# Scores of a gated recurrence by matmuls of 32 array columns, in place of 128, 64 and 32

## The chip, the cores and the metric

One core of a Trainium2 chip runs one kernel. The metric is device time in microseconds (us) of one execution. TensorE (PE) multiplies and loads its weights (PEld), VectorE (DVE), ScalarE (ACT) and GpSimd (POOL) do the rest, SyncE (SP) issues most of the DMAs.

## What is computed

The reference is an encoder trunk of two layers on 1024 tokens of width 1024, in float32. Both layers hold a bidirectional gated linear recurrence in chunks (`bidirectional_gated_scan`): four heads of 128 keys and 256 values in layer 0, twelve heads of 128 and 128 in layer 1. Cut to what matters here:

```python
b = jnp.cumsum(log_g, axis=2)                      # within a chunk
s = einsum('bnthk,bnshk->bnhts', q * exp(b - ref), k * exp(ref - b))
s = where(tril, s, 0.0)                            # scores within a chunk
o = einsum(s, v) + einsum(q * exp(b), state)       # per direction
```

The forward result and the flipped backward one are added, less the diagonal that both hold. The change touches `s` alone.

## The kernel before

**Staging.** The input projection runs in blocks of 128 channels and 512 tokens (`project`, L217 to L220; three matmuls per 128 rows of the contraction, on values split in two exact parts). The mixers come one after another: four pairs of attention heads (to about 517 us), four `GlaHead`s (to about 950 us), twelve `HgrnHead`s (from about 1010 us). While a head's core runs, `merge` lays projection blocks and output products beside it by fixed windows. That list is the order of priority; the tile framework orders each engine's instructions by it ahead of time, and lets an instruction that its plan finds ready pass one that it finds not ready. On the chip every engine's program is fixed.

**The core of a head** (`ScanHead.core`) does, for direction d (1 backward, 0 forward) and half hf of the tokens, in the order (1,1), (1,0), (0,0), (0,1): `prep` (gate products on ACT, DVE and POOL), `keys` (transposes at L760, state products at L769), `scores`, and for d = 0 then `output` (L820 to L824). So `scores` is called 4 times in each of 16 heads, 64 times.

**`scores`** makes, for 4 tiles of 128 tokens, X[s, t] of 128 by 128, in one PSUM bank of tag "s" (two buffers). Within 32 tokens the operands `ki`, `qi` serve; between the two 32-token pieces of a half tile `k1`, `q1` (scaled by products of gates, against overflow); between the two 64-token halves of a tile `k2`, `q2`. L794 multiplies each whole tile: 4 matmuls of 128 weight columns by 128 moving columns. L796 writes over the block between the halves (4 of 64 by 64), L801 over the blocks between the pieces (8 of 32 by 32, alternately at two of the four places of 32 array columns that lie 64 apart). Then one instruction moves the bank to `S`: for d = 1 a copy on ACT (L804), for d = 0 a masked copy on DVE (L806). All operands are float32, for which the program on PE holds two weight loads and two matmuls for each matmul of the source: the 256 of L794 stand as 512 in the trace. `S` is read by L820.

Of the kernel before, what the change touches and what calls it, by code (L numbers as in the profile page):

```python
# [55 lines left out]
def merge(*streams):  # L56
    """Units of several streams side by side; a stream (units, start, end) is spread over that part of the whole."""
    todo = []
    for units, a, b in streams:
        todo += [(a + (b - a) * (i + 0.5) / len(units), n, u) for n, (i, u) in enumerate(enumerate(units))]  # L60
    return [u for _, _, u in sorted(todo, key=lambda t: t[0])]


def emit(units):
    """Runs the units; the weights of each block load while the block before it is in use."""
    blocks, first = [], {}
    for i, u in enumerate(units):
        b = getattr(u, "block", None)
        if b and b not in blocks:
            blocks.append(b)  # L70
            first[b] = i
    for i, u in enumerate(units):
        b = getattr(u, "block", None)
        if b:
            for nb in blocks[blocks.index(b):][:2]:
                if nb is b or not any(getattr(v, "fence", False) for v in units[i:first[nb]]):
                    nb.load()
        u()


class Block:
    """Columns f0..f0+n of a projection; evac(ps, half) takes each half of the tokens out of PSUM."""
# [17 lines left out]
class Phase:  # L100
    """A pool that holds one phase's tiles."""
# [14 lines left out]
class Trunk:  # L116
# [15 lines left out]
    def set_mode(self):  # L132
        """Loads the table set that has both exp and ln."""
        self.guard = self.nc.scalar.preload_act_table_set("natural_log_exp_and_others").ins

    def act(self, *args, **kw):
        """An exp or ln; it keeps clear of the sigmoid batches."""
        with self.tc.issue_after(self.guard):
            self.last = self.nc.scalar.activation(*args, **kw).ins  # L139

    def sigmoids(self, fns, after):
        """A batch of sigmoids behind the last exp and behind `after`, then back to exp and ln."""
        prev = [i for i in (self.last, after) if i is not None]
        with self.tc.high_priority(offset=3000):
            for f in fns:
                with ExitStack() as st:
                    for p in prev:
                        st.enter_context(self.tc.issue_after(p))
                    prev = [f().ins]
            with self.tc.issue_after(prev[0]):  # L150
                self.set_mode()
# [4 lines left out]
    def load_w(self, w, f0, n):  # L156
        """Columns f0..f0+n of w [D, F] as two exact parts, a list of [P, n] for each k tile."""
# [27 lines left out]
    def load_wout(self, w, f0, nb, c0, nc_):  # L185
        """Rows f0..f0+128 nb, columns c0..c0+nc_ of w as two exact parts [P, nb, nc_]; nb nc_ = 1024."""
        h = self.wp.tile([P, nb, nc_], F32R, tag="woH", name="woH", bufs=1)
        lo = self.wp.tile([P, nb, nc_], F32R, tag="woL", name="woL", bufs=1)
        for g in range(2):
            raw = self.wp.tile([P, HALF], F32, tag="wraw", name="wraw", bufs=2)  # L190
            if nb == 2:
                src, hs, ls = w[f0 + g * P:f0 + (g + 1) * P, c0:c0 + nc_], h[:, g, :], lo[:, g, :]
            else:
                gs = slice(g * HALF, (g + 1) * HALF)
                src, hs, ls = w[f0:f0 + P, gs], h[:, 0, gs], lo[:, 0, gs]
            self.nc.sync.dma_start(raw, src)
            with self.tc.high_priority(offset=3000):
                self.nc.scalar.copy(hs, raw)  # L198
                self.nc.vector.tensor_tensor(ls, raw, hs.bitcast(F32), op=ALU.subtract)  # L199
        return h, lo  # L200

    def project(self, w, hf, m):
        """Channel-major projection of one half of the tokens: PSUM [m, 512]."""
# [19 lines left out]
    def out_units(self, w, ys, f0, hf, held):  # L223
        """z += y @ w[f0:...] for 4 token tiles; ys = [(yH, yL)] blocks of 128 features [P, 512 tokens]."""
# [29 lines left out]
    def final_units(self, w, f0, ys, norm, banks, reload):  # L254
        """The last product of the layer for one half of the tokens: z and y @ w meet in PSUM, for norm(i, halves).

        Returns a function of the half: the units that take z there for the first two tiles, and the others.
        """
# [46 lines left out]
    def transpose_x(self, i):  # L305
        """Token tile i of x, in z [P, D] -> columns of x^T, in two exact parts."""
# [12 lines left out]
    def after_x(self, fn):  # L319
        """A unit whose work on ACT and DVE stays behind the transposed input."""  # L320
        def run():
            with self.tc.issue_after(self.lastact), self.tc.issue_after(self.lastdve):
                fn()
        return run

    def ln_params(self, pool, tags, gain, bias):
        """Gain and bias of a layer norm on all partitions, in halves."""
# [8 lines left out]
    def layer_norm(self, pool, i, params, direct=False, src=None):  # L336
        """LayerNorm of token tile i into z; z, or the halves `src`, hold (alpha x + y) / alpha."""
# [27 lines left out]
class Item:  # L365
    """One unit of the mixers: the first `ne` of its projection blocks come early, the others late."""
# [10 lines left out]
    def units(self, ns, evac=None):  # L377
        """Units of the blocks ns whose values are not parked."""
# [13 lines left out]
    def spill(self, pool, tag, bufs, which):  # L392
        """Units for the (block, half) pairs of `which` ahead of this item's phase; the values wait in DRAM."""
# [37 lines left out]
class AttnPair(Item):  # L431
    """Two heads of the dilated attention.

    Tokens are taken as t = 4 j + r. A tile of queries has one residue r and one half h of the j; it meets
    A: the four residues of its own half, B: its own residue in the other half,
    C: the 16 nearest j of the other half in every residue (its own one masked, as B has it).
    """
# [12 lines left out]
    @staticmethod  # L450
    def edge(g):
        """The 16 positions of half g next to the other half."""
        return slice(112, 128) if g == 0 else slice(0, 16)
# [63 lines left out]
    def core(self):  # L517
# [4 lines left out]
        def strip(j):  # L522
            """Bias of every block, each run of keys reversed."""
# [119 lines left out]
class ScanHead(Item):  # L643
    """Bidirectional gated linear recurrence of one head: channel-major operands, token-major values."""
# [9 lines left out]
    def raw(self, dst, tag, bufs, scale=1.0):  # L654
        """Evacuation as it is, but for a factor."""
# [10 lines left out]
    def ev_v(self, vb):  # L666
        """Evacuation of values."""
# [8 lines left out]
    def tok_v(self, vt, hf, vb):  # L676
        """Values [128 channels, 512 tokens] -> token-major."""
# [8 lines left out]
    def prep(self, d, hf):  # L686
        """Gate products of 512 tokens for direction d (0 forward, 1 backward)."""
# [65 lines left out]
    def keys(self, d, hf):  # L753
        """State increments and states of 4 token tiles."""
# [29 lines left out]
    def scores(self, d, hf):  # L784
        """S^T[s, t] within 4 token tiles, built from three levels of blocks."""
# [5 lines left out]
        X = T.ps.tile([P, 4, P], F32, tag="s", name="s", bufs=2)  # L791
        for t in range(4):
            ts = slice(t * P, (t + 1) * P)
            mm(X[:, t, :], r["ki"][:, ts], r["qi"][:, ts], start=True, stop=True)  # L794
        for t in range(4):
            mm(X[64 * first:64 * first + 64, t, 64 * last:64 * last + 64],  # L796
               r["k2"][:, t].rearrange("p a c -> p (a c)"), r["q2"][:, t].rearrange("p a c -> p (a c)"),
               start=True, stop=True)
        for n in range(8):
            s0, t0 = 64 * (n % 2) + 32 * ev, 64 * (n % 2) + 32 * od  # L800
            mm(X[s0:s0 + 32, n // 2, t0:t0 + 32], r["k1"][:, n, :], r["q1"][:, n, :], start=True, stop=True)  # L801
        dst = self.S[:, hf * 4:hf * 4 + 4, :]
        if d == 1:
            nc.scalar.copy(dst, X)  # L804
        else:
            nc.vector.copy_predicated(out=dst, mask=T.mask.unsqueeze(1).broadcast_to([P, 4, P]), data=X)  # L806

    def output(self, hf):
        """o^T of 4 token tiles, normalised and gated, in two exact parts."""
# [84 lines left out]
class GlaHead(ScanHead):  # L894
# [20 lines left out]
    def ev_lr(self, ps, hf):  # L915
        """The low-rank gate inputs of every head, as stacked exact parts."""
# [8 lines left out]
    def gates(self):  # L925
        """Up-projection of the gates, as stacked exact parts."""
# [26 lines left out]
    def activate(self, d):  # L953
        """SiLU of the output gates."""
# [35 lines left out]
class HgrnHead(ScanHead):  # L990
# [25 lines left out]
    def out_half(self, hf):  # L1016
        """The output product of two heads, beside the second one."""
        return super().out_half(hf) if self.mate else []
# [11 lines left out]
    def activate(self, d):  # L1030
        """Sigmoids and SiLUs of what direction d needs; the output gate's may come apart."""
# [28 lines left out]
def trunk_kernel(tc, x, w_in_ab, gla_gate_up, gla_gate_bias, gla_norm, w_out_ab, w_in_c, hgrn_lower_bounds,  # L1060
                 hgrn_norm, w_out_c, rel_bias, ln_gain, ln_bias, onehot, ident, mask, out):
    nc = tc.nc
    with ExitStack() as ctx:
# [59 lines left out]
        def bias_line(q):  # L1123
            """Bias and log multiplicity of 512 of the distances."""
# [51 lines left out]
        def step(items, i, after=None, spill=()):  # L1176
            """Item i's core; beside it its late projections, the next item's early ones, the last item's product.

            After the last item come its own product, `after` for the token tiles of each finished half and `spill`.
            """  # L1180
# [66 lines left out]
def shape_constants():  # L1247
    """Tables that depend on the shapes alone."""
# [32 lines left out]
```

## Time and profile before

| | us |
|---|---|
| median of 3 runs (2070.28, 2071.64, 2073.94) | 2071.64 |
| span of the profiled execution | 2070.0 |
| PE busy in it | 2026.0 (98%) |
| DVE busy | 1304.6 (63%) |
| ACT busy | 1012.3 (49%) |
| POOL busy | 308.4 (15%) |

The profiled span is 1.6 us below the median and 0.3 us below the lowest run. "Busy" joins all instructions of an engine; matmuls overlap in the pipeline, so that a duration of 275 ns says little of the pace. The pace is read from starts: how long a run of n equal matmuls takes, less the last one's own duration, over n - 1.

### The profile page before, as it was taken

What the parts mean: (1) busy time and instruction counts of PE and PEld (TensorE: products, weight loads), DVE (VectorE), ACT (ScalarE), POOL (GpSimd) and SP (SyncE); (2) the same over time, 40 slices, a digit from 0 to 9 for tenths busy, and PEclk for the clock granted to TensorE, in tenths of its full rate; (3) what the DMA queues carried; (4) which work ended last, traced back from release to release, by engine and by line L of the source; (5) the groups of instructions that cost most, each with busy time, mean ns of one, the idle gap of its engine ahead of it and who ended that gap; (6) DMA issues with size and microseconds to landing.
All of it is one profiled execution on the core that took longest, in us unless ns stands there. A gap on an engine that the chain in (4) does not pass through costs nothing.

```text
span 2070.0 us, 29623 instructions
## 1 busy us (share of the span) xinstructions
PE 2026.0 (98%) x11103; PEld 1590.7 (77%) x11103; DVE 1304.6 (63%) x2727; ACT 1012.3 (49%) x1844; POOL 308.4 (15%) x838
## 2 busy tenths in 40 slices
PE   8999999999999999998999999999999999999998
PEld 6777676777787878876788788878878887887885
DVE  4677778776676565567675745555664464656467
ACT  4555555543544344344555444435444553544463
POOL 0100000100111011012222111111211111211124
PEclk9999999999999999999999999999999999999999
DMA  5311111211211112111311111111111111111112
GB/s 141 78 35 44 30 40 26 48 52 52 69 36 42 52 32 71 42 51 41 118 37 41 52 46 36 37 57 32 42 61 32 41 36 56 32 42 52 36 52 82
DMA packets 141258, 103.47 MB, mean 50 GB/s; under 512 B 14517, under 2 KB 122933, under 8 KB 141115
## 3 DMA queue, kind: packets, MB, share of 16 engines
q1 hardware_dynamic: 129355, 89.44, 14.7%
q0 software_dynamic: 3968, 9.77, 2.0%
q10 hardware_dynamic: 7792, 2.37, 0.5%
q8 instruction: 87, 1.43, 0.3%
q14 instruction: 56, 0.46, 0.1%
HBM read 93.71 MB, written 7.85 MB: 49 GB/s over the span
## 4 chain that ended last, share of the span: by engine, by line
PE 63%; DVE 4%; ACT 3%; issue 2%; POOL 1%; DMA 0%; DVEq 0%; ACTq 0%; POOLq 0%
PE pj L218 13%; PE pj L219 13%; PE pj L220 13%; PE kv L769 3%; PE s L794 2%; PE po L240 2%; PE po L241 2%; PE po L242 2%; PE s L796 2%; PE o L820 2%; PE o L822 1%; PE o L824 1%; PE tr L760 1%; PE s L801 1%; PE tr L683 1%
## 5 line engine op out<-in xcount | busy, mean ns | idle before, releaser
L218 PE MATMUL pj<-xH,wH 128*128 128x512 f32 x1600 | 649.1, 406 | 3.7 <-ACT vt L490 1.1
L219 PE MATMUL pj<-xL,wH 128*128 128x512 f32 x1600 | 642.9, 402 | 0.0
L220 PE MATMUL pj<-xH,wL 128*128 128x512 f32 x1600 | 640.9, 401 | 0.0
L218 PEld LDWEIGHTS pj<-xH,wH 128*128 128x128 f32 x1600 | 300.9, 188 | 73.8 <-ACT vt L490 2.8
L220 PEld LDWEIGHTS pj<-xH,wL 128*128 128x128 f32 x1600 | 300.9, 188 | 67.0 <-issue 2.4
L219 PEld LDWEIGHTS pj<-xL,wH 128*128 128x128 f32 x1600 | 301.1, 188 | 63.5 <-issue 1.7
L181 DVE TENSOR_TENSOR wL<-wraw,wH 128x512 fp32r<-128x512 f32 x210 | 146.6, 698 | 201.5 <-ACT wH L180 174.4
L180 ACT CAST wH<-wraw 128x512 fp32r<-128x512 f32 x210 | 129.9, 619 | 225.6 <-PE pj L219 191.7
L714 POOL TENSOR_TENSOR eT<-gE 128x16 f32<-128x16 f32 x64 | 36.2, 566 | 1106.6 <-ACT gE L139 1106.6
L245 DVE TENSOR_TENSOR z<-z,po 128x512 f32<-128x512 f32 x200 | 135.9, 683 | 79.9 <-PE po L242 77.8
L240 PE MATMUL po<-woH,yH 128*128 128x512 f32 x336 | 135.9, 409 | 0.9 <-ACT yH L618 0.4
L241 PE MATMUL po<-woL,yH 128*128 128x512 f32 x336 | 133.8, 398 | 1.4 <-DVE woL L199 1.4
L242 PE MATMUL po<-woH,yL 128*128 128x512 f32 x336 | 131.3, 393 | 0.0
L198 ACT CAST woH<-wraw 128x512 fp32r<-128x512 f32 x80 | 47.5, 617 | 94.1 <-PE po L242 43.8
L830 ACT ACTIVATE tmp<-o 128x512 f32<-128x512 f32 x40 | 23.9, 597 | 129.4 <-PE o L822 71.7
L661 ACT ACTIVATE F<-pj 128x512 f32<-128x512 f32 x62 | 36.8, 593 | 94.9 <-PE pj L220 94.9
L769 PE MATMUL kv<-v,k3T 128*128 128x128 f32 (+1 forms) x448 | 79.0, 311 | 1.1 <-ACT k3T L763 0.7
L240 PEld LDWEIGHTS po<-woH,yH 128*128 128x128 f32 x336 | 62.4, 188 | 22.9 <-ACT woH L198 5.3
L694 DVE TENSOR_TENSOR_SCAN g<-restart,g 128x512 f32<-128x512 uint8 x64 | 78.0, 1219 | 1.8 <-ACT g L139 1.2
L241 PEld LDWEIGHTS po<-woL,yH 128*128 128x128 f32 x336 | 63.2, 188 | 16.0 <-DVE woL L199 5.3
L242 PEld LDWEIGHTS po<-woH,yL 128*128 128x128 f32 x336 | 63.2, 188 | 14.0 <-DVE yL L849 1.1
L769 PEld LDWEIGHTS kv<-v,k3T 128*128 128x128 f32 x448 | 61.4, 190 | 16.0 <-ACT k3T L763 7.7
(226 smaller groups left out, 3581.0 us busy)
## 6 DMA issues: line engine op xcount, KB each, us to landing
wraw<-in_w_in_c_dram SPq DMA_DIRECT2D x130, 256.0 KB
wraw<-in_w_in_ab_dram SPq DMA_DIRECT2D x80, 256.0 KB
wraw<-in_w_out_c_dram SPq DMA_DIRECT2D x44, 256.0 KB
wraw<-in_w_out_ab_dram SPq DMA_DIRECT2D x40, 256.0 KB
strip<-line POOLq DMA_DIRECT2D x8, 448.0 KB, 5.3
park<-sp SPq DMA_DIRECT2D x13, 256.0 KB
out_dram<-z SPq DMA_DIRECT2D x6, 512.0 KB
z<-in_x_dram SPq DMA_DIRECT2D x4, 512.0 KB
```

The lines of the kernel that those rows point to most:

```text
L180: self.nc.scalar.copy(h, raw)
L181: self.nc.vector.tensor_tensor(lo, raw, h.bitcast(F32), op=ALU.subtract)
L198: self.nc.scalar.copy(hs, raw)
L218: mm(ps[:m], wH, xH[:, k, :], start=(k == 0), stop=False)
L219: mm(ps[:m], wH, xL[:, k, :], start=False, stop=False)
L220: self.lastmm = mm(ps[:m], wL, xH[:, k, :], start=False, stop=(k == last)).ins
L240: mm(ps, yH[:, ts], h, start=(b == 0), stop=False)
L241: mm(ps, yH[:, ts], lo, start=False, stop=False)
L242: mm(ps, yL[:, ts], h, start=False, stop=(b == nb - 1))
L245: self.nc.vector.tensor_tensor(zs, zs, ps, op=ALU.add)
L694: nc.vector.tensor_tensor_scan(run, T.restart, run, 0.0, op0=M, op1=ALU.add)
L769: nc.tensor.matmul(kv[:, j, :], k3T[:, t, :], self.v[:, hf * 4 + t, :], start=True, stop=True)
```

## The change

`scores` makes the same S from matmuls of 32 weight columns only, 32 of the source for each call instead of 16 (64 weight loads and 64 matmuls on PE instead of 32 and 32). For each tile `far` makes the block between the halves in two strips of 32 by 64, `near` the two blocks between pieces (32 by 32 each), `own` the four blocks on the diagonal, where the strip of the second piece (in the direction's order) takes 64 columns and that of the first 32. No block is written twice. The order in a tile goes round the four places of 32 array columns. The blocks that the mask or the other direction replaces are no longer made. The move to `S` is cut in two, 64 partitions each: one instruction of 4 by 128 columns and one of 4 by 64. Elsewhere only docstrings are gone.

```diff
     def scores(self, d, hf):
...
         X = T.ps.tile([P, 4, P], F32, tag="s", name="s", bufs=2)
+        def block(t, s0, t0, n, k, q):
+            mm(X[s0:s0 + 32, t, t0:t0 + n], k, q, start=True, stop=True)
+        def far(t, i):
+            k2, q2 = (r[x][:, t].rearrange("p a c -> p (a c)") for x in ("k2", "q2"))
+            block(t, 64 * first + 32 * i, 64 * last, 64, k2[:, 32 * i:32 * i + 32], q2)
+        def near(t, i):
+            n = 2 * t + i
+            block(t, 64 * i + 32 * ev, 64 * i + 32 * od, 32, r["k1"][:, n, :], r["q1"][:, n, :])
+        def own(t, i, e):
+            s0 = 64 * i + 32 * e
+            t0, n = (s0, 32) if e == ev else (64 * i, 64)
+            block(t, s0, t0, n, r["ki"][:, t * P + s0:t * P + s0 + 32], r["qi"][:, t * P + t0:t * P + t0 + n])
         for t in range(4):
-            ts = slice(t * P, (t + 1) * P)
-            mm(X[:, t, :], r["ki"][:, ts], r["qi"][:, ts], start=True, stop=True)
-        for t in range(4):
-            mm(X[64 * first:64 * first + 64, t, 64 * last:64 * last + 64],
-               r["k2"][:, t].rearrange("p a c -> p (a c)"), r["q2"][:, t].rearrange("p a c -> p (a c)"),
-               start=True, stop=True)
-        for n in range(8):
-            s0, t0 = 64 * (n % 2) + 32 * ev, 64 * (n % 2) + 32 * od
-            mm(X[s0:s0 + 32, n // 2, t0:t0 + 32], r["k1"][:, n, :], r["q1"][:, n, :], start=True, stop=True)
+            far(t, ev), far(t, od), own(t, last, ev), own(t, last, od)
+            near(t, first), own(t, first, od), near(t, last), own(t, first, ev)
         dst = self.S[:, hf * 4:hf * 4 + 4, :]
-        if d == 1:
-            nc.scalar.copy(dst, X)
-        else:
-            nc.vector.copy_predicated(out=dst, mask=T.mask.unsqueeze(1).broadcast_to([P, 4, P]), data=X)
+        for i in range(2):
+            ss = slice(64 * i, 64 * i + 64)
+            cs = slice(0, P) if i == first else slice(64 * last, 64 * last + 64)
+            if d == 1:
+                nc.scalar.copy(dst[ss, :, cs], X[ss, :, cs])
+            else:
+                mask = T.mask[ss, cs].unsqueeze(1)
+                nc.vector.copy_predicated(out=dst[ss, :, cs], data=X[ss, :, cs],
+                                          mask=mask.broadcast_to([64, 4, cs.stop - cs.start]))
```

## Rows read from the trace of the kernel before

**Rows 1.** The page: span, and each engine's busy time, share, instructions.

```profile
span 2070.0 us, 29623 instructions
PE 2026.0 (98%) x11103; PEld 1590.7 (77%) x11103; DVE 1304.6 (63%) x2727; ACT 1012.3 (49%) x1844; POOL 308.4 (15%) x838
```

**Rows 2.** Windows of the HGRN and GLA stages: length, then each engine's busy us.

```profile
1010.00:2012.00 1002.00, 998.45 (x5854) 812.17 (x5853) 571.40 (x1086) 486.31 (x816) 169.00 (x527) 1.00 0.15 46
517.00:950.00 433.00, 424.28 (x2332) 336.07 (x2332) 271.96 (x479) 190.35 (x341) 57.28 (x196) 0.99 0.17 48
```

**Rows 3.** Timeline of PE, one call: start us, length us, line, count.

```profile
1141.13 1.05 PE L794 MATMUL s<-qi,ki 128*128 128x128 f32 x8
1142.12 0.68 PE L796 MATMUL s<-q,k 128*64 128x64 f32 x8
1142.73 0.45 PE L801 MATMUL s<-q,k 128*32 128x32 f32 x16
1143.10 0.50 PE L218 MATMUL pj<-xH,wH 128*128 128x512 f32 x1
```

**Rows 4.** Timeline of PE, a call with state products between.

```profile
1152.29 1.06 PE L794 MATMUL s<-qi,ki 128*128 128x128 f32 x8
1153.19 0.93 PE L769 MATMUL kv<-v,k3T 128*128 128x128 f32 x6
1154.05 0.68 PE L796 MATMUL s<-q,k 128*64 128x64 f32 x8
```

**Rows 5.** Timeline of PE's weight loads, one call.

```profile
1122.28 0.97 PEld L794 LDWEIGHTS s<-qi,ki 128*128 128x128 f32 x8
1123.37 0.54 PEld L796 LDWEIGHTS s<-q,k 128*64 128x64 f32 x8
1123.98 0.33 PEld L801 LDWEIGHTS s<-q,k 128*32 128x32 f32 x16
```

**Rows 6.** Groups by line and form: count, busy us, mean ns, idle before.

```profile
L794 PEld LDWEIGHTS s<-qi,ki 128*128 128x128 f32 x512 | 64.5, 191 | 7.3 <-DVE ki L987 2.0 <-issue 1.4 <-PE tr L838 1.0
L796 PEld LDWEIGHTS s<-q,k 128*64 128x64 f32 x512 | 34.7, 137 | 9.7 <-issue 1.3 <-DVE k L749 0.7 <-DVE g L979 0.7
L801 PE MATMUL s<-q,k 128*32 128x32 f32 x1024 | 28.7, 199 | 0.0
L801 PEld LDWEIGHTS s<-q,k 128*32 128x32 f32 x1024 | 21.5, 112 | 5.1 <-issue 1.0
```

**Rows 7.** Lines L760 and L769, 1489.6 to 1491: the sequencer's own instruction.

```profile
L760 PEldq EVENT_SEMAPHORE  x1: 51/51/51, 1489.8 to 1489.8; - x1
...
L769 PEldq EVENT_SEMAPHORE  x1: 51/51/51, 1490.1 to 1490.1; - x1
```

**Rows 8.** Line L837, 1951 to 1954.5, and a window of that stretch.

```profile
L837 PEldq EVENT_SEMAPHORE  x1: 51/51/51, 1951.4 to 1951.4; - x1
L837 PEld LDWEIGHTS tr<-sqH,ones x1: 186/186/186, 1954.2 to 1954.2; 128*128 128x128 f32 x1
...
1951.43:1954.20 2.77, 2.77 (x19) 2.22 (x18) 0.71 (x2) 1.22 (x2) 0.00 (x0) 1.00 0.00 0
```

**Rows 9.** Groups by form: moves to S, and half-size neighbours.

```profile
L804 ACT COPY S<-s 128x512 f32<-128x512 f32 x32 | 18.8, 591 | 13.1 <-PE s L801 13.1
L602 ACT COPY pB<-tr 128x256 f32<-128x256 f32 x32 | 11.8, 370 | 17.1 <-DVE pC L601 17.0
L806 DVE COPY_PREDICATED S<-mask,s 128x512 f32<-128x512 uint32 x32 | 23.5, 734 | 15.5 <-PE s L801 14.1
L750 DVE TENSOR_TENSOR q<-qi,F3q 128x512 f32<-128x512 f32 x64 | 43.9, 686 | 16.0 <-PE o L822 16.0
L748 DVE TENSOR_TENSOR q<-qi,Gq 128x256 f32<-128x256 f32 x64 | 26.8, 419 | 0.0
```

**Rows 10.** Timeline: the move to S and its first reader, after rows 3.

```profile
1143.23 0.73 DVE L806 COPY_PREDICATED S<-mask,s 128x512 f32<-128x512 uint32 x1
1144.84 0.38 PE L820 MATMUL o<-S,v 128*128 128x128 f32 x2
```

**Rows 11.** Timeline: the move to S and its first reader, at the layers' border.

```profile
955.35 0.71 DVE L806 COPY_PREDICATED S<-mask,s 128x512 f32<-128x512 uint32 x1
956.11 0.49 PE L820 MATMUL o<-S,v 128*128 128x128 f32 x2 [0.51 <-DVE S L806]
```

**Rows 12.** Timeline: DVE's last operand k2 and PE's L794, one call.

```profile
1062.74 0.41 DVE L749 TENSOR_TENSOR k<-ki,Gk 128x256 f32<-128x256 f32 x1
1064.41 1.05 PE L794 MATMUL s<-qi,ki 128*128 128x128 f32 x8
```

## The prediction

> **What bounds the kernel now.** I read the page first: PE is busy 2026.0 of 2070.0 us, DVE 63%, ACT 49% [rows 1]. Then the windows by stage, because that share is an average: in the HGRN stage PE is busy 998 of 1002 us at full granted clock, in the GLA stage 424 of 433, while DVE has 571 and 272 [rows 2]. So where 61 of the 64 calls of `scores` lie, PE sets the pace, and what a call gets shorter on PE is gained nearly one for one. (The three others lie at the border of the layers and in the last stretch.) Then the timeline of single calls. In 46 of the 64 the three parts follow each other as in [rows 3]: L794 0.99 us, L796 0.61, L801 0.37, together 1.97 us. In the other 18 something comes between L794 and L796, as the state products do in [rows 4].
>
> **What a call costs, by its paces.** L794's eight take 0.90 us when an operation of the same 128 columns follows [rows 4] and 0.99 when one of 64 columns does [rows 3]: 0.09 is the price of entering another width. The loads of weights, by starts [rows 5], follow each other at (0.97 - 0.19) / 7 = 111 ns for 128 by 128, at (0.54 - 0.14) / 7 = 57 ns for 64 by 64 (durations in [rows 6]). A line through both gives 30.5 ns for a matmul of 32 moving columns on one place of the array. But L801's sixteen follow at (0.33 - 0.11) / 15 = 14.5 ns [rows 5, 6], half of that: its two places, which the program takes alternately, work side by side, each at its own 30 ns. Sixteen at 15 ns are 0.24; the other 0.13 of the 0.37 us are entry and end of the block. Going back to 128 columns costs the next matmul some 0.11 us more (an exposed weight load of that pace, 111 ns), before and after the change alike.
>
> **The change on PE.** Removed for each call: 1.97 us. Added: 64 matmuls of 32 weight columns, per tile four of 64 moving columns and four of 32 in the source, each twice on PE. If four places work side by side as two do in L801, the fullest place has per tile one of 64 and two of 32: 2 x (57 + 30.5 + 30.5) = 236 ns, 0.94 us for four tiles. That is the lower bound of the block.
>
> The other limit is the supply of instructions, now 128 in one block where L801 had 32. Two rows price it. The sequencer of PE executes an own instruction for L760 at 1489.8 and for L769 at 1490.1 us [rows 7]; in program order 16 loads and matmuls lie between (the four transposes and four projection matmuls, most of which run after 1490.1). So 16 are sent in 0.2 to 0.3 us: 13 to 19 ns each. And the sequencer runs ahead by a limited count: for L837 it acts at 1951.4, 2.8 us before L837 loads, and 19 matmuls and 18 loads touch that stretch, four of them already under way [rows 8]: 33 stand ready. So of 128 instructions 33 are ready and 95 come at 13 ns: 1.24 us, more than 0.94. I take 13, since the second of those instructions may itself have waited, which makes 13 to 19 an upper bound; with 19 the block is 1.8 us. From below, if supply costs nothing, it is 0.94.
>
> The Trainium skill (TensorE: Matmul & The Clock Gate, the table at its head) gives PE a queue of 64 instructions; the trace shows 33. With 64 ready the block would be 0.94, and the call 0.30 us shorter than in my sum.
>
> A call that is one block: 0.09 entry + 1.24 + 0.13 = 1.46 us instead of 1.97, -0.51; x 46 = -23.5 us. The 18 others: part of them has k2, q2 not ready when L794 starts, part has state products put between. I take it that their 32 matmuls also fall in two blocks: `own`, where the fullest place has one matmul of 64 columns per tile, 4 x 2 x 57 = 0.46 us (supply: 64 - 33 = 31 x 13 = 0.40, less), and `far` with `near`, 4 x 2 x (57 + 30.5) = 0.70. With two entries, ends and returns, 0.46 + 0.70 + 2 x (0.09 + 0.13 + 0.11) = 1.82 us. Before, such a call is 0.90 + 0.09 + 0.61 + 0.37 + 0.11 = 2.08 us [rows 3, 4]. So -0.26 x 18 = -4.7. Together **-28 us** on PE.
>
> **The rest of the change.** The first matmul is now `far`, which needs k2, the last operand but one of `prep`; L794 needed only ki, qi. In all 46 whole calls k2 was finished well before L794 starts; the tightest is [rows 12], 1063.15 against 1064.41. So no stall there: price 0, cover 1.26 us; without it PE would stand at most the 0.99 us by which the need for k2 moves ahead, in each call that loses it. What the plan of the tile framework makes of the new lengths I can't read from a trace; its order may get better or worse anywhere. PE has only 4 us idle in the HGRN stage and 9 in the GLA stage [rows 2], so a better order gains little, and a worse one may cost: I take +1, with -3 and +15 as its ends. The move to S is two instructions instead of one: on ACT 370 ns more (the copy of 256 columns) [rows 9] x 32 = 12 us, on DVE 734 less the difference of the 512- and 256-column products, 686 - 419 [rows 9], so 467 ns more x 32 = 15 us. Both engines have 37% or more free [rows 1]. On the path lies only S's lateness: L806 ends at 1143.96, L820 starts at 1144.84 [rows 10], 0.88 us later, so 0.47 is covered; the wait is the tightest at the layers' border, where L820 waits already [rows 11]: +0.5 there, and if the cover were gone everywhere 0.47 x 32 = 15 us. I take +1 in all. Matmuls end a call earlier by 0.5 us, so the PSUM bank comes free no later than now.
>
> **Sum.** 2070.0 - 28 + 1 + 1 = 2044 for the profiled span; the median lies 1.6 us above the span that I sum against. So 2046 us, -1.2%. Its own range is 2038 to 2056 (order and S's lateness at their ends, supply at 12 to 15 ns).
>
> **The rivals.**
>
> *Supply costs less.* Then the fullest place decides, 0.94 us: 46 x 0.30 = 14 us more, 2032. For it: 13 is an upper bound. Against: L801's 32 instructions ran from what stood ready, so no row shows a faster sustained supply.
>
> *Starts in program order.* If a matmul can't start before the one ahead of it in the program, then the second of each pair waits for the first on its place, and only the next pair's first runs beside it. Each matmul of the source then costs one pace, not two in parallel: 4 x (57 + 30.5) = 350 ns a tile, 1.40 us, and 0.09 for the three tile borders where the same place follows itself; call 1.49 + 0.22 = 1.71, -0.26 x 46 = -12, the other 18 calls about 0 (1.40 + 0.66 = 2.06 against 2.08). With +2: 2062. L801 has just two places, so this order and free places give it nearly the same pace, and [rows 5] can't decide. The Trainium skill says so (TensorE: Matmul & The Clock Gate, Part 3, What overlaps and what doesn't): matmuls start and end in program order. By that rule the time is this rival's.
>
> *Neighbouring places exclude each other* (the slower end). L801 shows two places 64 columns apart; the new order goes to neighbours. If neighbours take turns, 32 + 32 matmuls at 57 and 30.5 ns are 2.8 us, a call 3.02, +1.05 x 46, and +1.4 x 18 for the split ones: +74, 2147. It decides from the point where a matmul takes 1.97 - 0.22 = 1.75 us / 64 = 27 ns in the mean; my forecast has 19, full exclusion 44. Supply at 19 ns would just reach that point (1.8 us). Against: two places run at full pace each in L801, and nothing in the rows ties a place to its neighbour.
>
> *The gain is given back.* The order of instructions, which the plan makes anew, puts waits on PE that eat 20 to 35 us: 2068 to 2080. For it: PE is 98% busy in an order that leaves 4 us idle in 1002, so most new orders are worse. Against: DVE and ACT keep 37% and 51% free.
>
> **How the numbers follow.** Forecast (2038 to 2056) 0.44; supply costs less (2026 to 2038) 0.12; program order (2056 to 2067) 0.17; given back 0.15, of which 0.08 within 0.2% (2067.5 to 2075.8) and 0.07 above; neighbours exclude each other, fully or in part (2080 to 2147), 0.12. A measurement of this kernel tells about 0.2% from no change. So faster 0.73, same 0.08, slower 0.19. The range leaves out 0.04 below and about 0.14 above: 2030 to 2080.
>
> **What would show it.** The new matmuls stand in one group, 4096 of them. A whole call should last 1.35 to 1.5 us from the first new matmul to the next operation; 0.95 to 1.1 speaks for a cheaper supply, 1.6 for program order, near 3 for exclusion. If supply binds, the pace falls within a block, fast for about 33 instructions and then some 26 ns for each load and matmul; under the other cases it is even. PE's busy time should fall by about 28 us and its idle time stay; if idle time grows instead, the order gave the gain back, and the waits name the engine. The moves to S should show 64 on ACT and on DVE with 0.37 to 0.6 and 0.47 to 0.73 us, and L820's successor should wait for S no more than now. The prediction is wrong if a block takes over 1.75 us, or if the waits of PE grow by more than 10 us.

## The result, and the profile after

| | before | after |
|---|---|---|
| median, on one chip | 2072.8 us | **2051.6 us** (2049.2 to 2052.5) |
| ratio, 95% interval | | 0.9888 (0.9877 to 0.9900) |
| profiled span | 2070.0 us | 2049.6 us |
| PE busy / idle within the span | 2026.0 / 44.0 us | 1985.2 / 64.4 us |

The forecast was 2046 us, 2030 to 2080. The time is in the range and the sign is right, but the table's last row already says that the sum behind it isn't: PE's busy time fell by 40.8 us where I had 28, and its idle time, for which I had +2, rose by 20.4. The two errors nearly cancel, so that the time came out near the forecast is in part luck.

The page of the kernel after (beside [rows 1]): span, then each engine's busy time, share and instructions.

```profile
span 2049.6 us, 33800 instructions
PE 1985.2 (97%) x13151; PEld 1538.2 (75%) x13151; DVE 1323.0 (65%) x2759; ACT 1023.6 (50%) x1876; POOL 320.9 (16%) x838
```

Windows of the HGRN and the GLA stage after, as in [rows 2]: length, then busy us of PE, PEld, DVE, ACT and POOL. PE, idle for under 4 us in 1002 of HGRN before, is now idle for 13 in 953.

```profile
1047.00:2000.00 953.00, 940.16 (x7269) 750.53 (x7267) 567.92 (x1086) 481.68 (x819) 175.31 (x515) 1.00 0.15 44
517.00:943.00 426.00, 410.65 (x2803) 322.18 (x2801) 272.46 (x481) 193.74 (x347) 55.38 (x199) 0.99 0.18 51
```

One whole call after, which answers [rows 3]: PE's timeline (start, length, line, count). The first of the 64 new matmuls starts at 1131.32, the last about 1132.26, the next operation at 1132.39: 1.07 us, 0.94 of it from the first start to the last. Before it was 1.97.

```profile
1131.32 0.25 PE L795 MATMUL s<-q,k 128*32 128x64 f32 x2
1131.33 0.25 PE L795 MATMUL s<-qi,ki 128*32 128x32 f32 x3
...
1132.23 0.23 PE L795 MATMUL s<-qi,ki 128*32 128x32 f32 x2
1132.39 0.50 PE L218 MATMUL pj<-xH,wH 128*128 128x512 f32 x1
```

Groups by line and form after: first the moves to S (ACT L821, DVE L824, beside [rows 9]), then PE's operations whose idle time grew (busy us, mean ns | idle us before, and what ended it). Before, the same three groups had 1.1, 2.3 and 0.5 us of idle time.

```profile
L821 ACT COPY S<-s 64x512 f32<-64x512 f32 x32 | 18.6, 582 | 0.4
L821 ACT COPY S<-s 64x256 f32<-64x256 f32 x32 | 11.6, 361 | 10.5 <-PE s L795 10.5
L824 DVE COPY_PREDICATED S<-mask,s 64x512 f32<-64x512 uint32 x32 | 23.1, 722 | 8.6 <-PE s L795 8.6
L824 DVE COPY_PREDICATED S<-mask,s 64x256 f32<-64x256 uint32 x32 | 14.4, 451 | 0.8
L769 PE MATMUL kv<-v,k3T 128*128 128x128 f32 x336 | 48.8, 285 | 9.5 <-DVE stb L781 4.8 <-ACT k3T L763 2.1 <-DVE gt L697 1.4
L760 PE MATMUL tr<-ident,k 128*128 128x128 f32 x224 | 35.2, 274 | 6.7 <-DVE k L738 6.7
L839 PE MATMUL o<-S,v 128*128 128x128 f32 x320 | 62.6, 278 | 2.6 <-DVE S L824 2.6
```

**Where the gain came from and went.** Each of the 64 calls begins with L760's transposes, so their starts cut the span at the same places in every kernel. The table gives the length of each stretch and, behind the stroke, PE's idle time in it; the last four kernels are experiments told below. The first 536 to 541 us hold no call, the code there is the same in all kernels, and the length still varies by 5 us between executions (536.8 us before, 539.7 after): compare the stretches, not the spans alone.

| us | GLA | border of the layers | HGRN | end |
|---|---|---|---|---|
| before | 412.4 / 7.0 | 95.0 / 6.9 | 979.4 / 4.4 | 46.4 / 8.4 |
| after | 405.3 / 12.2 | 101.5 / 10.6 | 956.2 / 13.3 | 46.8 / 9.8 |
| old_two_moves | 415.2 / 10.2 | 102.3 / 10.4 | 979.3 / 3.7 | 46.3 / 9.4 |
| second_bank | 405.2 / 12.0 | 101.7 / 10.7 | 952.3 / 7.2 | 46.8 / 9.8 |
| dve_one | 404.4 / 11.9 | 96.1 / 8.5 | 958.3 / 13.8 | 45.6 / 8.9 |
| bank_dve_one | 404.1 / 11.4 | 95.3 / 7.7 | 954.1 / 7.4 | 45.6 / 8.9 |

So the change won 7.1 us in GLA and 23.2 in HGRN, and lost 6.5 at the border. PE's busy time (length less idle time) fell by 45.4 us in GLA, HGRN and the end together; at the border it rose by 2.8, and in the first stretch, by chance, by 1.8. Three places gave gain back: the border, some 9 us of new idle time in HGRN, some 5 in GLA.

### The profile page after: what moved, and what is told of

Read it like the earlier page. It is cut to its first block, busy times and chain, and to the rows that moved or that the text cites. A ratio compares the mean times of both kernels' runs of the same rounds, so it can differ in the third digit from the quotient of the medians.

```text
span 2049.6 us, 33800 instructions
## 1 busy us (share of the span) xinstructions
PE 1985.2 (97%) x13151; PEld 1538.2 (75%) x13151; DVE 1323.0 (65%) x2759; ACT 1023.6 (50%) x1876; POOL 320.9 (16%) x838
## 4 chain that ended last, share of the span: by engine, by line
PE 46%; DVE 6%; ACT 5%; issue 2%; DMA 2%; POOL 1%; DVEq 0%; ACTq 0%; POOLq 0%
PE pj L218 10%; PE pj L219 10%; PE pj L220 10%; PE kv L769 2%; DVE g L694 2%; PE po L240 2%; PE po L241 2%; PE po L242 2%; PE s L795 2%; PE o L839 1%; DMA wraw<-in_w_out_c_dram 1%; PE o L841 1%; PE o L843 1%; DMA wraw<-in_w_in_c_dram 1%; PE tr L683 1%
## 5 line engine op out<-in xcount | busy, mean ns | idle before, releaser
L714 POOL TENSOR_TENSOR eT<-gE 128x16 f32<-128x16 f32 x64 | 31.6, 493 | 1071.1 <-ACT gE L139 1071.1
L198 ACT CAST woH<-wraw 128x512 fp32r<-128x512 f32 x80 | 47.5, 617 | 94.9 <-PE po L242 43.8
L769 PE MATMUL kv<-v,k3T 128*128 128x128 f32 (+1 forms) x448 | 79.7, 312 | 9.6 <-DVE stb L781 4.8
L769 PEld LDWEIGHTS kv<-v,k3T 128*128 128x128 f32 x448 | 60.5, 190 | 28.2 <-ACT k3T L763 13.6
L795 PEld LDWEIGHTS s<-q,k 128*32 128x32 f32 x2048 | 62.5, 110 | 19.5 <-issue 16.5
L795 PE MATMUL s<-qi,ki 128*32 128x64 f32 (+1 forms) x2048 | 74.7, 213 | 0.0
```

The source lines that it names most:

```text
L769: nc.tensor.matmul(kv[:, j, :], k3T[:, t, :], self.v[:, hf * 4 + t, :], start=True, stop=True)
L795: mm(X[s0:s0 + 32, t, t0:t0 + n], k, q, start=True, stop=True)
```

## The experiments

Theories that stood after the comparison: the block is set by its fullest place, and the 20 us of idle time come from the longer moves to S (A), or from the shorter block and the new order alone (B).

**one_move**: the places of the change, one move per bank. For that the half with fewer columns also writes the quarter that the mask leaves out.

```diff
             t0, n = (s0, 32) if e == ev else (64 * i, 64)
+            if i == last:
+                t0, n = min(t0, 64 * first), n + 64
...
-        for i in range(2):
...
+        if d == 1:
+            nc.scalar.copy(dst, X)
+        else:
+            nc.vector.copy_predicated(out=dst, mask=T.mask.unsqueeze(1).broadcast_to([P, 4, P]), data=X)
```

> The four places of the changed kernel, but every bank moved to S in one go as in the kernel before. For that the places of the half that has fewer columns also write the quarter that the mask leaves out (64 columns more on two places of each token tile, so that all four places stream 128 columns; 64 matmuls per call as in the change). Both theories expect the block of a call to stay at 0.94 us from the first start to the last and 1.07 to the next operation, since the busiest place had 128 columns per tile before too; if something else than the busiest place sets the block (the sum of the columns), it grows by a third, to about 1.4. Theory A, the 20 us of new TensorE idle time come from the two moves (ACT 0.94 in place of 0.57, DVE 1.17 in place of 0.71 per call): TensorE's idle time falls from 64 back to 44 to 50 us and the time to 2030 to 2038. Theory B, they come from the shorter block and the order of the work around it alone: 2047 to 2055.

Measured: 2052.3 us, ratio 0.9901 (0.9886 to 0.9915). A whole call stayed at 1.07 us although a third more columns run: the fullest place sets it, not the sum. The time is B's, but the stretches say that B is not why: the border went back from 101.5 to 94.9 us, and HGRN grew from 956.2 to 966.4. There PE now waits at L769 10.1 us for DVE (11 times, 0.9 us each, once per head) and 6.4 us for ACT. So the moves do cost, and something else took it back.

**old_two_moves**: the matmuls of before with the two moves of the change (the inverse edit).

> The matmuls of the kernel before, with the two moves per bank of the changed one: the price of the second move without the places. Theory A, the moves make the new waits: 13 to 20 us slower than the kernel before, 2085 to 2093. Theory B, the moves lie beside TensorE and the waits come from the shorter block: 2070 to 2077.

Measured: 2083.0 us, ratio 1.0045 (1.0032 to 1.0058), some 9 us slower than before: between the two theories, close to A. Of the 12.0 us between the two profiled spans 7.3 lie at the border, 2.8 in GLA and 2.1 in the first stretch, which the edit doesn't touch; HGRN has none. With the two moves kept, the places alone are thus worth 2083.0 - 2051.6 = 31 us.

**own_first**: the same matmuls, those of `qi` and `ki` ahead.

```diff
-            far(t, ev), far(t, od), own(t, last, ev), own(t, last, od)
-            near(t, first), own(t, first, od), near(t, last), own(t, first, ev)
+            own(t, last, od), own(t, first, od), own(t, last, ev), own(t, first, ev)
+        for t in range(4):
+            far(t, ev), far(t, od), near(t, first), near(t, last)
```

> The same 64 matmuls of a call in another order: first the 16 of each place's own block (32 or 64 columns) for all four tiles, which need qi and ki alone, then those of k2, q2 and k1, q1. The busiest place has 64 columns per tile in the first half and 64 in the second. If places run on their own as far as the 33 instructions ready reach, the block is 0.94 to 1.1 us and the time is 2050 to 2058; if an instruction waits for those ahead of it in the program, a place with 32 columns waits for one with 64 and the block grows to 1.2 to 1.5, the time to 2059 to 2078. If the new waits hang on which operands come last, TensorE's idle time of 64 us changes by more than 5 either way; else it stays within that.

Measured: 2052.5 us, a whole call 1.15 us to the next operation, PE idle 60.6 us: places run on their own, and the order within a call matters little as long as all four are served in turn.

**twice**: every matmul of a call issued twice.

```diff
-        for t in range(4):
+        for t in (0, 1, 2, 3, 0, 1, 2, 3):
```

> Each of the 64 matmuls of a call is issued twice (the second writes the same values): what a call's TensorE time is worth at the end. Two calls that follow each other without a gap took 2.02 us for 128 matmuls in the changed kernel, so the call grows by 0.95 us and TensorE's busy time by 61 us. If TensorE's work is on the path everywhere, the time is 2051.6 + 61 = 2113. If the 20 us of new idle time are waits that other engines set and a longer block hides, part of it is hidden: 2090 to 2105, with TensorE's idle time down from 64 to 45 to 55 us. If instruction supply binds over 256 instructions, the call grows by 1.2 or more and the time passes 2125.

Measured: 2122.3 us, PE busy 64 us more, idle 70.7. The whole calls take 2.02 us, as forecast, so instruction supply doesn't bind over 256 instructions either. The time grew by 71, not 61: what the longer block adds passes through in full, nothing is hidden here, and the new order adds waits of its own (L769 waits 11.4 us for DVE in HGRN, 11 times). PE is still the bound of the kernel after.

**place_by_place**: one place's matmuls for all tiles, then the next place's.

```diff
+        for t in range(4):
+            far(t, ev), near(t, first), own(t, first, ev)
+        for t in range(4):
+            far(t, od), own(t, first, od)
+        for t in range(4):
+            near(t, last), own(t, last, ev)
+        for t in range(4):
+            own(t, last, od)
```

> The same 64 matmuls of a call, one place after the other (12 for the first place, then 8, 8 and 8 or so), in place of side by side: what the interleaving is worth. If matmuls of other places start only in program order one after the other, the call takes the sum of all columns, 384 per tile or about 2.6 us, and the time is 2052 + 1.5 x 64 = 2148 or more. If TensorE looks ahead over the 33 instructions (16 matmuls) that stand ready, each place begins while the one before it still runs, and the call takes 1.3 to 2.0 us: 2066 to 2112. If place by place costs nothing, the interleaving did not make the gain, the narrower columns did: 2048 to 2056.

Measured: 2124.9 us. PE's timeline of a call in this kernel:

```profile
1066.50 0.36 PE L795 MATMUL s<-q,k 128*32 128x64 f32 x4
...
1067.24 0.36 PE L795 MATMUL s<-q,k 128*32 128x64 f32 x5
...
1068.53 0.58 PE L795 MATMUL s<-qi,ki 128*32 128x32 f32 x9
1069.03 0.50 PE L218 MATMUL pj<-xH,wH 128*128 128x512 f32 x1
```

1069.03 - 1066.50 = 2.53 us, nearly the serial sum; all the gain of the change is the interleaving. (The time rose by 73 us, not by 64 x 1.46 = 93; PE's idle time is 11 us smaller here, 3.4 us in HGRN where it was 13.3, and L769 has no wait there at all.) The single starts show how far TensorE reaches past a place that is taken: the first place's 24 matmuls start at 0 to 0.94 us, the second's first at 0.857, ahead of just the last three of the first (0.879, 0.911, 0.943). (In the fence, the last tile has five matmuls of q and k from 1067.24 on, where the tiles ahead have four.) Third and fourth place begin in the same way, each past three. That the program on PE holds them in the kernel's order is not seen in the trace; that it is three each time, and that one of the three is the second of the two matmuls for one of the source, speaks for it.

**second_bank** and **second_bank_o**: a second PSUM bank for the state increments. In HGRN after, PE's L769 waits for DVE's update of the state once per head. DVE's timeline and then PE's, at one of the ten places:

```profile
1132.12 0.32 DVE L781 SCALAR_TENSOR_TENSOR stb<-stb,dec,kv 128x128 f32<-128x128 f32 x1
...
1132.46 1.22 DVE L694 TENSOR_TENSOR_SCAN g<-restart,g 128x512 f32<-128x512 uint8 x1
1133.60 0.32 DVE L781 SCALAR_TENSOR_TENSOR stb<-stb,dec,kv 128x128 f32<-128x128 f32 x1
```

```profile
1134.06 0.91 PE L769 MATMUL kv<-v,k3T 128*128 128x128 f32 x6 [0.48 <-DVE stb L781]
```

The increments of both halves share one bank, and the first half's last update stands behind a scan of 1.22 us. The kernel before at the same place, with the same operations on PE between the transposes and L769, only with the longer block:

```profile
1133.83 0.34 DVE L781 SCALAR_TENSOR_TENSOR stb<-stb,dec,kv 128x128 f32<-128x128 f32 x1
1134.32 0.91 PE L769 MATMUL kv<-v,k3T 128*128 128x128 f32 x6
```

There too PE starts 0.15 us behind the update, but it had work until then: the longer block brought it there as late as DVE. The same line waited 0.3 us for stb in the whole kernel, after the change 4.8. In place_by_place, with the same order there and a block of 2.53 us, the wait is gone.

```diff
-            kv = T.ps.tile([P, per, V], F32, tag="kv", name="kv", bufs=1)
+            bank = "tr" if V == P and (d, hf) in ((1, 0), (0, 1)) else "kv"
+            kv = T.ps.tile([P, per, V], F32, tag=bank, name="kv", bufs=1)
```

> The changed kernel, but in the last stage (value width 128) the state increments kv of each direction's second half of the tokens go to the bank of the tag tr, which their own k3 transposes just left, and not to the one bank of the tag kv, which the first half's three DVE updates still hold. Theory A, that bank is a wait that the shorter block brought to light: the 4.8 us (DVE stb) and 1.4 us (DVE gt) of waits of L769 go, and TensorE gains 6 to 8 us: 2043 to 2047. Theory B, DVE is late there whatever bank is used, and TensorE meets it at the next step (the next transposes to tr, the output): the waits change their line and the time stays at 2049 to 2055.

> The same with the tag o, whose two banks the output uses and not the next transposes. Theory A: 2043 to 2047 again, without a new wait at the transposes of tr. Theory B: 2049 to 2055, with new waits at L769 or at the users of o (the output product and the output of a half).

Measured: 2044.7 us (0.9857, 0.9837 to 0.9876) and 2045.5 us (0.9860, 0.9845 to 0.9874). Waits of the line after (now L770) in HGRN, tag tr: us and times. Both DVE entries, 6.2 us, are gone, and PE's idle time there fell from 13.3 to 7.2. The stretch itself got only 3.9 us shorter (second_bank), since PE's busy time rose by 2.2: ten more calls are cut in two.

```profile
its engine sat idle before it (us, times) until:
  ACT k3T L763: 2.5, 5
```

**old_second_bank**: the same edit in the kernel before.

> The kernel before with the second bank for kv (tag tr) in the last stage, nothing else: was the wait that the second bank takes away there before the change? Theory A, it came with the change (before, L769 waited for nothing of DVE's in that stage, and for k3T only 0.7 us): no gain, 2070 to 2077. Theory B, the one bank costs as much in either kernel: 6 to 8 us faster than before, 2065 to 2068.

Measured: 2071.6 against 2074.7 us, ratio 0.9989 (0.9980 to 0.9999): at most 0.2%. PE's idle time in HGRN fell by 0.8 us here and by 6.1 after the change, so the wait came with the change; the stretch fell by 2.4 here and 3.9 there, so not all that the bank is worth did.

**second_bank_one**: one_move with the second bank (tag o).

> The same (tag o) with one move per bank to S and the two filled quarters, where L769 waited 13.0 us for DVE and 7.0 for ACT's k3T in the last stage (excess over the natural pace). Theory A: 10 to 16 us less than its own 2052.3, 2036 to 2042. Theory B: 2049 to 2055.

Measured: 2055.0 us, no gain; my theory A failed here. The wait for the bank went, and PE met DVE one step later: L760 waits 10.7 us for k3 (L738) in HGRN, 11 times, where one_move had none. In that plan PE meets DVE 1 us early once per head, with the one bank or with two.

**dve_one** and **bank_dve_one**: only DVE's masked move is one again (quarters filled for d = 0 alone); ACT keeps two. Why DVE: at the border its two halves of a move don't follow each other. The kernel after, DVE and PE:

```profile
951.06 0.70 DVE L824 COPY_PREDICATED S<-mask,s 64x512 f32<-64x512 uint32 x1
951.97 0.69 DVE L317 TENSOR_TENSOR xL<-kv,xH 128x512 fp32r<-128x512 f32 x1 [0.21 <-ACT xH L316]
952.58 0.27 DVE L345 BATCH_NORM_AGGREGATE mv<-st 128x2 f32<-128x12 f32 x2
952.76 0.64 DVE L199 TENSOR_TENSOR woL<-wraw,woH 128x512 fp32r<-128x512 f32 x1
953.43 0.44 DVE L824 COPY_PREDICATED S<-mask,s 64x256 f32<-64x256 uint32 x1
953.93 0.49 PE L839 MATMUL o<-S,v 128*128 128x128 f32 x2 [2.62 <-DVE S L824]
...
1013.35 1.12 PE L312 MATMUL tr<-ident,z 128*128 128x128 f32 x4 [2.71 <-POOL z L362]
```

The second half stands behind a layer norm's work, so PE waits 2.62 us for S where it waited 0.51 before [rows 11]. 60 us later it waits 2.71 for the norm's last tiles (L312).

The first of these two waits is not what the border lost. It takes the place of another: before, and in dve_one, PE waited a few us later for the norm's first tiles; after, these are there when PE comes. In the order before, dve_one, after:

```profile
961.52 0.66 PE L312 MATMUL tr<-ident,z 128*128 128x128 f32 x4 [2.68 <-POOL z L362]
954.47 0.66 PE L312 MATMUL tr<-ident,z 128*128 128x128 f32 x4 [2.48 <-POOL z L362]
957.83 0.67 PE L312 MATMUL tr<-ident,z 128*128 128x128 f32 x4
```

From the border's start to its sixth group of four at L312 it is 18.0 us before, 17.8 in dve_one and 17.8 after. All that the border lost lies behind: 77.0 us before, 78.3 in dve_one, 83.7 after, with 2.6, 3.8 and 5.9 us of idle time.

> The changed kernel with the second bank, and the masked move of the forward direction on DVE in one go (with the two quarters filled so that it may read the whole bank); the two moves of ACT stay. DVE has 32 x 0.47 = 15 us less to do. Theory A, DVE's queue is what TensorE waits for in the two scan stages: TensorE's idle time falls by 4 to 10 us and the time to 2035 to 2041. Theory B, the plan puts TensorE's next work earlier by as much and it meets DVE at another place (as with both moves in one): 2043 to 2056.

> The changed kernel with DVE's masked move in one go and ACT's two moves, without the second bank: the fourth corner beside 2051.6 (neither), 2044.7 (second bank) and 2038.2 (both). Theory A, the two gains are separate waits and add up: 2044 to 2047, with the waits of L769 for DVE's stb still there (about 5 us in the last stage). Theory B, DVE's shorter queue already frees the one bank earlier, so the second bank adds little on top: 2037 to 2041. Theory C, the gain of DVE's single move needs the second bank, since TensorE only meets the bank earlier (as when both engines had one move): 2049 to 2054.

Measured: 2038.2 us for both edits, ratio 0.9819 (0.9806 to 0.9833), the best of all; 2044.2 us for DVE's move alone, 0.9860 (0.9843 to 0.9876). Set beside 2051.6 and 2044.7, the two edits add up: 6.9, 7.5 and together 13.4 us (in ratios to the kernel before on the same chip 0.31, 0.28 and 0.69%). In dve_one L769 still waits the 4.8 us for stb, ten times: two separate waits, theory A of that run. The same place in dve_one:

```profile
948.50 0.70 DVE L820 COPY_PREDICATED S<-mask,s 128x512 f32<-128x512 uint32 x1
949.26 0.49 PE L843 MATMUL o<-S,v 128*128 128x128 f32 x2 [0.51 <-DVE S L820]
```

The border is back at 96.1 us, and the wait of 2.71 is gone. Theory A of bank_dve_one gave the time, but its place was too broad: the gain lies at the border, not in the two scan stages, whose stretches moved by 1 to 2 us. Of the 5.4 us between after and dve_one at the border 2.1 are idle time; the other 3.3 are busy time, most of which the clock accounts for. Windows of 5 us, PE's busy us right behind the length, the granted clock third from the end; the kernel after, from the wait on:

```profile
1010.00:1015.00 5.00, 1.75 (x7) 0.90 (x5) 3.07 (x4) 2.44 (x4) 3.32 (x2) 0.76 0.32 105
1015.00:1020.00 5.00, 4.97 (x17) 4.20 (x18) 1.38 (x2) 1.26 (x3) 2.17 (x4) 0.56 0.80 230
```

and dve_one at about the same work:

```profile
1003.00:1008.00 5.00, 4.71 (x25) 3.65 (x23) 2.44 (x5) 2.24 (x5) 2.38 (x2) 1.00 0.19 52
1008.00:1013.00 5.00, 4.77 (x23) 3.80 (x23) 1.78 (x4) 1.95 (x4) 2.17 (x4) 1.00 0.59 165
```

In the first window PE was idle for 3.25 us, and in the next the granted clock is 0.56 in the mean, so for most of it at the lower of its two levels (1.2 and 2.4 GHz); that window alone lacks 5 x (1 - 0.56) = 2.2 us of full clock. old_two_moves shows the same pair of waits (2.62 and 2.71 us) and the same clock (0.77, 0.54), so the second move makes them under either set of matmuls. The later wait is 2.70 or 2.71 us in every kernel here with DVE's two moves except twice, and in those with one the longest at L312 behind the sixth group is 1.12. How a second move makes the norm's last tiles late 60 us on was not shown. A part of the difference between after and dve_one (1.6 us) lies in the first stretch, which the edit doesn't touch.

**bank_own_first**: the second bank, and own_first's order in the GLA stage alone.

> The changed kernel with the second bank (2044.7), and in the stage of value width 256 the own blocks of a call first, then those of k2, q2, k1 and q1. In that stage TensorE waits 7.4 us for k3 of DVE at L760, 1.0 to 1.4 a time, where the kernel before had the 0.9 us of its 128-column matmuls (qi and ki alone) to do. Theory A, those waits are there because the change's first block needs the last operands: about half of them (2.6 us in own_first) go and the split calls cost 16 x 0.2 = 3 us, so 2043 to 2047, no gain. Theory B, the split of the call costs more than that (each half is bound by its own busiest place and ends with its own drain): 2048 to 2053.

Measured: 2048.5 us (0.9871, 0.9855 to 0.9886), theory B. L760's wait for k3 in GLA fell from 6.2 to 3.5 us, but the stage went from 405.2 to 409.3: PE's busy time there rose by 4.4 us, so calls in two halves cost more than that.

## Why the prediction was right, and where it was not

The time lies in the range and PE sets it, as forecast; but two terms were mis-sized in opposite directions. The prediction had named as a sign of being wrong that PE's waits grow by more than 10 us. They grew by 20.4.

**What bounds the kernel**: right. With every call doubled the time rose by the whole of it.

**The block, 1.24 us**: wrong, it is 0.94, my lower bound, which the rival "supply costs less" took. The step that failed is the price of 13 ns an instruction. I had called it an upper bound, since the sequencer's instruction may itself have waited, and then used it as the value. In twice, 256 instructions ran in 2.02 us; with 33 ready, that is at most 2.02 / 223 = 9 ns. That rival asked for 14 us more, -42 on PE; measured -40.8, as close as that by chance (-45.4 in GLA, HGRN and the end, +2.8 at the border, +1.8 in the first stretch). Its time of 2032 would have come if idle time had stayed: 2070.0 - 40.8 = 2029.2 of span, and with the 20.4 us of new idle time 2049.6.

**Starts in program order** and **places that exclude each other**: both refuted by the call of 1.07 us (1.62 to the next operation and some 3 were forecast). The Trainium skill (TensorE: Matmul & The Clock Gate, Part 3, What overlaps and what doesn't) keeps matmuls in program order; for matmuls on different places this trace disagrees, by starts that pass three waiting ones (in place_by_place 0.857 us, ahead of 0.879, 0.911 and 0.943). The same run shows that it doesn't reach further.

**The split calls**, 18 forecast, 17 found: the price held. The pair of halves that HGRN has once per head takes 0.80 and 0.59 us from its first start to the next operation, 0.14 of the first idle; the sum had 0.83 and 0.59 for this, and 0.40 for entries and returns. But each half is two tiles, not `own` alone and `far` with `near`.

**Order, +1 us (at most +15)**: too small. HGRN's 6.2 us at the one bank are part of it. I had written that the bank comes free no later than now, and looked at the bank of the scores alone; which bank PE reaches before its reader is done I had not asked. GLA's 5 us more sit mostly before L760 (waits for k3: 6.7 us after against 2.2). In the kernel before, L794 stood right ahead of those transposes in six of the eight waits; its successor needs later operands. That this is the reason was not shown, since own_first's order was no test without a price of its own.

**Lateness of S, +1 us**: the sizes of the moves were right (ACT 582 + 361 - 591 = 352 ns more, forecast 370; DVE 722 + 451 - 734 = 439, forecast 467), and so was the place (the border, [rows 11]). The step that failed is that the second half follows the first at once. In DVE's queue a state update (L781) stands between the two in 24 of 32 pairs, and at the border a layer norm's work, 1.67 us. But that wait of 2.62 us only took the place of one at L312. What made 6.5 us of the 0.5 at the border came later, and the sum had no term for it: the wait of 2.71 us and the lower clock behind it, which come with DVE's second move. Elsewhere the cover held.

**The gain is given back**: in part. I had 20 to 35 us for it with 0.15, and took "DVE and ACT keep a third free" as evidence against. A share of free time says nothing on an order within a queue.

What stays open: how DVE's second move makes the later wait at the border, why the plan of one_move, with less work on DVE and ACT, makes HGRN 10 us longer than that of the change, and what GLA's waits for k3 need.

## What to carry to other kernels

When an engine that bounds the kernel gets a stretch shorter, ask of each buffer that it reaches sooner who still reads it, and in which order that reader's queue stands; free time on the reader is no answer. When one operation is cut in two, look where the second stands in its queue, and compare the whole stretch: the wait that it makes may replace another, and the loss may come later. And a bound is not a value: where a cost was only bounded from above, the sum should be made at both ends before one is taken.

## What the runs showed of the hardware

Matmuls of 32 columns run on four neighbouring places at full pace each: 64 take 1.07 us to the next operation side by side, 2.53 us one place after the other. TensorE starts a matmul on a free place past three that wait for a taken one, no further in any of the starts looked at here. Loads and matmuls came at 9 ns each or less over 256 instructions. In all 14 traces PE's sequencer stands at most 33 loads and matmuls ahead of the array, counted from its own instructions as in [rows 8]. At the layers' border the 5 us in which a wait of 2.71 us ends had a mean granted clock of 0.76, the next 5 us 0.56.
